# Out-projection of a decoder layer: its last two weight groups by seven block products of half width, sums on the vector engine

## The chip, the cores and the metric

One core of one Trainium2 chip runs the kernel. The engines named below are PE (TensorE, matmuls; PEld its weight loads), DVE (VectorE), ACT (ScalarE), POOL (GpSimd) and SP (SyncE, here only a DMA queue). The metric is the device time of one execution in microseconds; lower is better.

## The reference, cut to what matters

A layer takes `x` (512 tokens, 1024 features), normalises and modulates it, projects it, runs two head groups of attention, gates their outputs by SiLU, and projects back:

```python
y = jnp.concatenate([o_a.reshape(Bn, S, D_A) * jax.nn.silu(z_a.astype(jnp.float32)),
                     o_b.reshape(Bn, S, D_B) * jax.nn.silu(z_b.astype(jnp.float32))], axis=-1)
out = y.astype(x.dtype) @ w_out
return x + gate[:, None, :] * out
```

`y` is 512 x 1024, `w_out` 1024 x 1024, all float32. Only the product `y @ w_out` is computed in another way by the change. Everything ahead of it (input projection, sliding-window attention of group A, compressed, selected and windowed attention of group B) stays.

## The kernel before

Everything is held transposed: features on the 128 partitions, tokens along the free axis. `y` is eight tiles of 128 features x 512 tokens, `w_out` is cut into four weight groups `o0` to `o3` of 256 output features, each loaded as two halves of 512 KB (`load_next`, on SP's queue, one load for each `raw` buffer that comes free). The result is eight output tiles n = 0 to 7 of 128 features x 512 tokens.

Float32 accuracy comes from splitting each factor into a high part, rounded to the matmul's fp32r type, and a low part, the rest: `h = wh + wl`. The high part is an ACT copy, the low part a DVE subtraction (`split` for weights, L176 and L177; `make_y` for y, L810 and L811). A product is then three matmuls: wh by yh, wh by yl, wl by yh.

A weight group is split into four pieces of 128 x 512. `split_to` emits the splits six pieces ahead of the one that the matmuls use (`AHEAD`). `unit_col` makes one output tile: for each of the eight row tiles k of y, three matmuls of a 128 x 128 weight with 512 moving columns, accumulated in one PSUM bank; two pieces serve one output tile. The three banks of `PJ` take turns. After an output tile DVE computes `fin` = bank * gate + x (L1037), where x comes by a DMA on ACT's queue (`xr`), and SP stores it. The last tile, n=7, is done in two halves of 256 tokens so that the store behind the last matmul is short:

```python
for tok in ((slice(0, S),) if n < 7 else (slice(0, 256), slice(256, S))):
```

The y tiles 0 to 3 belong to head group A and are ready early. Tiles 4 to 7 belong to group B: `make_y` for row r runs when the attention of row r ends, or, where the gate of that row was not ready at that time, after all attention (the loop behind `stream.drain()`), from a copy `ob`.

The order of the work on each engine is not the order of the source text. A scheduler takes the instructions with their dependences and, in a simulated run, gives each engine the earliest one in the text whose inputs and buffers are ready. On the chip every engine then runs its own list in that fixed order and waits in front of an instruction whose inputs are late. Buffers come from pools: `t2` (tiles of 128 x 512, `NT2` of them: h, q, transposed probabilities, y), `rawp` (loaded weights), `pw` (split weights), and small ones (`W2`) for temporaries and `fin`.

## Time and profile before

| | |
|---|---|
| median of 3 runs | 311.42 us (311.38 to 311.58) |
| the profiled execution | 312.03 us on the device, span 309.4 us from the first to the last instruction |
| granted TensorE clock | 0.999 |
| busy | PE 302.0 us (98% of the span), PEld 255.2 (82%), DVE 241.6 (78%), ACT 194.9 (63%) |
| chain that ended last | PE 78%, DVE 11%, ACT 4%, DMA 3% |

The profile is one execution. A row of the timeline gives start, length, engine, line, operation and tiles (written from read); square brackets behind it give the idle time of the engine ahead of it and what released it. Lengths of matmuls overlap, since they are pipelined; the distance from start to start is the pace. A row of groups by shape has the count, the busy time, the mean length in ns, and the idle time ahead of the group. A row of stretches gives the busy time of each engine between two times of the span, then the granted clock, the DMA share and GB/s.

### The profile page before, as it was taken

Reading aid. Unit: us, or ns where it says so; the run is one execution under the profiler, and the core shown is the slowest. Engines: PE = TensorE matmul, PEld = TensorE weight load, DVE = VectorE, ACT = ScalarE, POOL = GpSimd, SP = SyncE. Lnnn points to the kernel's source line nnn. Section 1 sums busy time; section 2 is a strip of 40 time slices with the busy share of each in tenths; the row PEclk is TensorE's granted clock in tenths of the full one; section 3 lists DMA queues with packets and bytes.
Section 4 is the critical chain, followed back from the end, with each engine's and each line's share of the span. In section 5 each row is a group of like instructions: output and inputs, shape, how many; then the busy total and the mean of one; then the engine's idle time right before and its main releaser. Section 6 shows DMA issues by size and latency. Waiting matters only on the chain.

```text
span 309.4 us, 5849 instructions
## 1 busy us (share of the span) xinstructions
PE 302.0 (98%) x2119; PEld 255.2 (82%) x2119; DVE 241.6 (78%) x666; ACT 194.9 (63%) x472; POOL 4.1 (1%) x22
## 2 busy tenths in 40 slices
PE   8999999999999999999999999999999999999995
PEld 3678888788988999889887888888888888788885
DVE  5679998999967567898999999988789696544221
ACT  5686448668967675676936665869778877422000
POOL 0000000000000000000000000000000000000000
PEclk9999999999999999999999999999999999999999
DMA  7999969800390909170454004140420220254101
GB/s 252 382 407 408 406 202 251 307 0 0 117 328 13 293 4 263 45 271 2 154 182 158 20 2 138 65 138 3 136 71 0 68 70 2 68 172 135 68 34 68
DMA packets 28231, 44.11 MB, mean 143 GB/s; under 512 B 1787, under 2 KB 19612, under 8 KB 28204
## 3 DMA queue, kind: packets, MB, share of 16 engines
q1 hardware_dynamic: 26908, 41.57, 39.3%
q10 hardware_dynamic: 1296, 2.18, 2.3%
q8 instruction: 16, 0.26, 0.3%
q14 instruction: 11, 0.09, 0.1%
HBM read 41.61 MB, written 2.14 MB: 141 GB/s over the span
## 4 chain that ended last, share of the span: by engine, by line
PE 78%; DVE 11%; ACT 4%; DMA 3%; issue 1%; SPq 1%; DVEq 0%; ACTq 0%
PE pj L484 28%; PE po L949 8%; PE sq L292 8%; PE pj L474 8%; PE s L874 7%; PE pt L932 4%; PE skv L293 4%; PE pt L922 3%; PE s L603 3%; DVE qs L535 2%; DMA raw<-in_w_gate 2%; DVE raw L709 2%; DMA xTp<-in_xT 2%; DVE wl L177 1%; PE s L666 1%
## 5 line engine op out<-in xcount | busy, mean ns | idle before, releaser
L176 ACT ACTIVATE wh<-raw 128x512 fp32r<-128x512 f32 (+1 forms) x52 | 31.3, 635 | 18.0 <-PE pj L484 14.1
L474 PE MATMUL pj<-wl,hh 128*128 128x256 f32 (+1 forms) x128 | 36.8, 288 | 0.1
L474 PE MATMUL pj<-wh,hh 128*128 128x256 f32 (+1 forms) x128 | 37.0, 289 | 0.0
L474 PE MATMUL pj<-wh,hl 128*128 128x256 f32 (+1 forms) x128 | 36.5, 285 | 0.0
L177 DVE TENSOR_TENSOR wl<-raw,wh 128x512 fp32r<-128x512 f32 (+1 forms) x52 | 34.9, 690 | 1.8 <-ACT wh L176 1.7
L886 ACT ACTIVATE pp<-pp,nm 128x256 f32<-128x256 f32 (+2 forms) x48 | 29.3, 615 | 7.0 <-DVE nm L879 6.9
L484 PE MATMUL pj<-hl,wh 128*128 128x512 f32 x80 | 32.2, 402 | 0.0
L484 PE MATMUL pj<-hh,wl 128*128 128x512 f32 x80 | 32.0, 400 | 0.0
L484 PE MATMUL pj<-hh,wh 128*128 128x512 f32 x80 | 32.0, 400 | 0.0
L879 DVE CUSTOM_DVE_ANT_0 pp<-s,bias 128x256 f32<-128x256 f32 (+2 forms) x48 | 25.6, 553 | 4.1 <-PE s L874 3.6
L484 PE MATMUL pj<-yh,wl 128*128 128x512 f32 (+1 forms) x72 | 26.6, 370 | 0.0
L484 PE MATMUL pj<-yl,wh 128*128 128x512 f32 (+1 forms) x72 | 26.6, 369 | 0.0
L1037 DVE SCALAR_TENSOR_TENSOR fin<-pj,gate,xr 128x512 f32<-128x512 f32 (+1 forms) x9 | 6.2, 692 | 25.9 <-PE pj L484 25.9
L484 PE MATMUL pj<-yh,wh 128*128 128x512 f32 (+1 forms) x72 | 26.4, 371 | 0.0
L474 PEld LDWEIGHTS pj<-wl,hh 128*128 128x128 f32 x128 | 24.1, 188 | 0.6 <-DVE wl L177 0.3
L874 PE MATMUL s<-kTb,qs 128*128 128x256 f32 (+2 forms) x96 | 24.3, 356 | 0.0
L474 PEld LDWEIGHTS pj<-wh,hl 128*128 128x128 f32 x128 | 24.1, 188 | 0.2 <-issue 0.2
L474 PEld LDWEIGHTS pj<-wh,hh 128*128 128x128 f32 x128 | 24.1, 189 | 0.1
L907 DVE TENSOR_SCALAR pp<-pp,rr,grev 128x256 f32<-128x256 f32 (+2 forms) x48 | 21.0, 475 | 0.5
L933 ACT COPY ptT<-pt 128x384 f32<-128x384 f32 (+1 forms) x32 | 15.8, 528 | 6.0 <-PE pt L932 5.9
L534 ACT ACTIVATE qs<-pt 64x512 fp32r<-64x512 f32 x16 | 9.5, 592 | 13.4 <-PE pt L529 7.3
L484 PEld LDWEIGHTS pj<-hh,wh 128*128 128x128 f32 x80 | 15.1, 188 | 3.0 <-issue 0.2
(238 smaller groups left out, 721.4 us busy)
## 6 DMA issues: line engine op xcount, KB each, us to landing
ada_ring<-in_w_ada_rows SPq DMA_DIRECT2D x12, 512.0 KB, 7.2
raw<-in_w_cmp SPq DMA_DIRECT2D x8, 512.0 KB, 5.4
raw<-in_w_gate SPq DMA_DIRECT2D x8, 512.0 KB, 5.6
raw<-in_w_o SPq DMA_DIRECT2D x8, 512.0 KB, 4.2
wst_ring<-in_w_qkv_a SPq DMA_DIRECT2D x8, 384.0 KB, 7.7
xTp<-in_xT SPq DMA_DIRECT2D x8, 256.0 KB, 4.6
bias<-line_d SPq DMA_DIRECT2D x8, 256.0 KB, 4.1
raw<-in_w_q_b SPq DMA_DIRECT2D x4, 512.0 KB, 6.5
```

The lines of the kernel that those rows point to most:

```text
L176: ACT.activation(wh, src, AF.Copy)
L177: DVE.tensor_tensor(wl, src, wh.bitcast(F32), op=OP.subtract)
L292: PE.matmul(pj_q[tb], lt, w[:, 0:512], start=f, stop=l, skip_group_check=True)
L293: PE.matmul(pj_kv[tb // 2][:, tb % 2, :], lt, w[:, 512:768], start=f and tb % 2 == 0, stop=l, skip_group_check=True)
L474: PE.matmul(bank[:, t * n:(t + 1) * n], h[:, tb * 128:(tb + 1) * 128], w[:, k % 2, :], start=k == 0 and m == 0, stop=k == 7 and m == 2)
L484: PE.matmul(bank, w, h[:, tok], start=k == 0 and m == 0, stop=k == 7 and m == 2)
L874: PE.matmul(ps, qs[h][:, 128 * i:128 * i + 128], k[:, hl_, lo:lo + w], start=hl_ == 0, stop=hl_ == 1)
L879: DVE.tensor_tensor_reduce(out=P[:, g, 0:w], in0=ps, in1=bt, scale=1.0, scalar=init, op0=OP.add, op1=OP.min, accum_out=nm[:, g:g + 1])
L886: ACT.activation(P[:, g, 0:e], P[:, g, 0:e], AF.Exp, bias=nm[:, g:g + 1], scale=-1.0, accum_out=dn[:, g:g + 1])
L907: DVE.tensor_scalar(v, v, rr[:, g:g + 1], gates[:, g, br:br + 1], op0=OP.mult, op1=OP.mult)
L933: ACT.copy(T[:, 0:nb, :], rev(pt[:, 0:nb * 128].rearrange("p (b q) -> p b q", b=nb)))
L949: PE.matmul(o[64 * g:64 * g + 64, 128 * i:128 * i + 128], vb[:, 64 * g:64 * g + 64], sl["T"][g][:, b, :], start=first_of and b == 0, stop= ...
```

## The change

The groups `o2` and `o3` (output tiles 4 to 7) are computed by a two-by-two block scheme with seven products in place of eight. Split are the tokens (two halves of 256), the rows of y (tiles 0 to 3 and 4 to 7), and the output features of the group (two tiles of 128). So each weight group has four blocks of 512 rows x 128 features, held as 128 x 512 tiles (`11`, `12`, `21`, `22`), and y has four blocks of 512 rows x 256 tokens. Four of the products take sums of y blocks (`s1` to `s4`) and differences of weight blocks (`t1` to `t4`):

- `split_out` makes the pieces of a weight group in the order 11, t1, t2, 22, t3, 21, t4: for the t pieces one DVE subtraction of 128 x 512, then for every piece the high part on ACT and the low part on DVE. There are seven pieces for a group instead of four.
- `y_sums` is called for each of four rows r behind output tile 1 (for s1 and s2) and behind output tile 2 (for s3 and s4): two DVE operations of 128 x 256, an ACT high part and a DVE low part of 128 x 512. For this `yf` is kept, in pool `t2`.
- `out_product` runs 4 rows x 3 matmuls with 256 moving columns into one of three PSUM banks, r, v and w. Products that belong to the same running sum go on accumulating in the bank after it has been read: r takes four products (11·11, s2·t2, s3·t3, 22·t4), v two (s1·t1, s4·22), w one (12·21).
- Behind each product DVE adds its bank, times the gate, to half an output tile (256 tokens): seven such evictions for a group, four of them onto `xr` (the first for each of the four half-tiles), three onto what the half-tile already holds. Four stores of 128 KB for a group.
- Output tiles 0 to 3 are computed as before. The split of n=7 is gone with the tile's old form. `NT2` goes from 40 to 44, there is a pool `ot` of two 128 x 512 tiles for the differences, and `xr` has four buffers.
- The host layout of `w_o2` and `w_o3` puts each block in one contiguous piece; the bytes are the same.

```diff
@@ -26,7 +26,7 @@
 LINE = 640
 GW = 280
 AHEAD = 6
-NT2 = 40
+NT2 = 44
 WAIT_L, WAIT_M = 4, (0, 8)
 PER_A, PER_B = 3.6, (3.5, 1.6, 7)
 NEAR = 256
@@ -89,6 +89,7 @@
     t2 = ctx.enter_context(tc.tile_pool(name="t2", bufs=NT2))
     rawp = ctx.enter_context(tc.tile_pool(name="rawp", bufs=5))
     pw = ctx.enter_context(tc.tile_pool(name="pw", bufs=4))
+    ot = ctx.enter_context(tc.tile_pool(name="ot", bufs=2))
     sm = ctx.enter_context(tc.tile_pool(name="sm", bufs=2))
 
     def T2(dt, name):
@@ -153,18 +154,43 @@
             t = rawp.tile([128, 4, GW], F32, name="raw")
             if g[:4] == "gate":
                 raws[g, h] = t.rearrange("p a b -> p (a b)")[:, 0:D]
+            elif g in OUT:
+                raws[g, h] = t.rearrange("p a b -> p (a b)")[:, 0:D]
             else:
                 raws[g, h] = t[:, :, 0:A["w_" + g].shape[3]]
             SP.dma_start(raws[g, h], A["w_" + g][h])
 
-    COL = ("kv_cmp", "z_a0", "z_a1", "z_b0", "z_b1", "o0", "o1", "o2", "o3")
+    COL = ("kv_cmp", "z_a0", "z_a1", "z_b0", "z_b1", "o0", "o1")
+    OUT = ("o2", "o3")
+    BLOCKS = ("11", "t1", "t2", "22", "t3", "21", "t4")
     split_list = [(g, p) for g in ("kv_cmp", "kv_sel", "kv_win_g", "q_b0", "q_b1", "z_a0", "z_a1", "z_b0", "z_b1",
-                                   "o0", "o1", "o2", "o3") for p in range(4)]
+                                   "o0", "o1") for p in range(4)]
+    split_list += [(g, p) for g in OUT for p in BLOCKS]
     split_pos = {e: n for n, e in enumerate(split_list)}
     split_done = [0]
 
+    def split_out(g, p):
+
+        blocks = {f"{i + 1}{j + 1}": raws[g, i][:, 512 * j:512 * j + 512] for i in range(2) for j in range(2)}
+        wh, wl = (pw.tile([128, 2 * GW], F32R, name=n)[:, 0:512] for n in ("wh", "wl"))
+        if p in blocks:
+            src = blocks[p]
+        else:
+            a, b = {"t1": ("12", "11"), "t2": ("22", "t1"), "t3": ("22", "12"), "t4": ("21", "t2")}[p]
+            sums = raws[g, "t"] = raws.get((g, "t"), {})
+            src = sums[p] = ot.tile([128, 512], F32, name="ot")
+            DVE.tensor_tensor(src, *({**blocks, **sums}[n] for n in (a, b)), op=OP.subtract)
+        ACT.activation(wh, src, AF.Copy)
+        DVE.tensor_tensor(wl, src, wh.bitcast(F32), op=OP.subtract)
+        pieces[g, p] = [t.rearrange("p (k n) -> p k n", k=4) for t in (wh, wl)]
+        if p in ("t3", "t4"):
+            load_next()
+
     def split(g, p):
 
+        if g in OUT:
+            split_out(g, p)
+            return
         if g in COL:
             src = raws[g, p % 2][:, :, 128 * (p // 2):128 * (p // 2) + 128]
         else:
@@ -183,7 +209,7 @@
 
         while split_done[0] < min(len(split_list), split_pos[g, p] + ahead + 1):
             n, q = split_list[split_done[0]]
-            if not all((n, h) in raws for h in ((0, 1) if n in COL else (q // 2,))):
+            if not all((n, h) in raws for h in ((0, 1) if n in COL + OUT else (q // 2,))):
                 break
             split(n, q)
             split_done[0] += 1
@@ -800,15 +826,39 @@
         else:
             sz[n - 4] = z
 
-    yh, yl = {}, {}
+    yf, yh, yl, yp, sums_y = {}, {}, {}, {}, {}
+    TOK = (slice(0, 256), slice(256, 512))
+
+    def high_low(src, names):
+
+        h, l = (T2(F32R, n) for n in names)
+        ACT.activation(h, src, AF.Copy)
+        DVE.tensor_tensor(l, src, h.bitcast(F32), op=OP.subtract)
+        return h, l
 
     def make_y(c, o, z):
 
-        yf = W2("yf")
-        DVE.scalar_tensor_tensor(yf, o, 0.5, z, op0=OP.mult, op1=OP.mult)
-        yh[c], yl[c] = T2(F32R, f"yh{c}"), T2(F32R, f"yl{c}")
-        ACT.activation(yh[c], yf, AF.Copy)
-        DVE.tensor_tensor(yl[c], yf, yh[c].bitcast(F32), op=OP.subtract)
+        yf[c] = T2(F32, "yf")
+        DVE.scalar_tensor_tensor(yf[c], o, 0.5, z, op0=OP.mult, op1=OP.mult)
+        yh[c], yl[c] = high_low(yf[c], (f"yh{c}", f"yl{c}"))
+
+    def y_sums(r, second):
+
+        (a0, a1), (b0, b1) = ([yf[c][:, t] for t in TOK] for c in (r, 4 + r))
+        if not second:
+            s12 = sums_y[r] = T2(F32, "s12")
+            DVE.tensor_tensor(s12[:, TOK[0]], a1, b1, op=OP.add)
+            DVE.tensor_tensor(s12[:, TOK[1]], s12[:, TOK[0]], a0, op=OP.subtract)
+            src, names = s12, ("s1", "s2")
+            for n, c, e in (("11", r, 0), ("12", 4 + r, 0), ("22", 4 + r, 1)):
+                yp[n, r] = [x[c][:, TOK[e]] for x in (yh, yl)]
+        else:
+            src, names = W2("s34"), ("s3", "s4")
+            DVE.tensor_tensor(src[:, TOK[1]], b0, sums_y[r][:, TOK[1]], op=OP.subtract)
+            DVE.tensor_tensor(src[:, TOK[0]], a0, a1, op=OP.subtract)
+        t = high_low(src, ("ysh", "ysl"))
+        for n, e in zip(names, TOK):
+            yp[n, r] = [x[:, e] for x in t]
 
     def gen2():
         posts.append(cmp_attn())
@@ -1021,21 +1071,52 @@
     with in_order(tc, late, ACT.engine):
         xrs = []
         for n in range(2):
-            xrs.append(mp.tile([128, S], F32, name="xr", tag="qc", bufs=2))
+            xrs.append(mp.tile([128, S], F32, name="xr", tag="qc", bufs=4))
             ACT.dma_start(xrs[n], A["xT"][n])
-    for n in range(8):
+    for n in range(4):
         if n < 2:
             xr = xrs[n]
         else:
-            xr = mp.tile([128, S], F32, name="xr", tag="qc", bufs=2)
+            xr = mp.tile([128, S], F32, name="xr", tag="qc", bufs=4)
             ACT.dma_start(xr, A["xT"][n])
-        f = W2("fin")
-        for tok in ((slice(0, S),) if n < 7 else (slice(0, 256), slice(256, S))):
-            b = PJ()[:, tok]
-            for _ in unit_col(f"o{n // 2}", n % 2, b, (yh, yl), tok):
-                pass
-            DVE.scalar_tensor_tensor(f[:, tok], b, gate[:, n:n + 1], xr[:, tok], op0=OP.mult, op1=OP.add)
-            SP.dma_start(out[n][:, tok], f[:, tok])
+        f, b = W2("fin"), PJ()
+        for _ in unit_col(f"o{n // 2}", n % 2, b, (yh, yl)):
+            pass
+        DVE.scalar_tensor_tensor(f, b, gate[:, n:n + 1], xr, op0=OP.mult, op1=OP.add)
+        SP.dma_start(out[n], f)
+        if n in (1, 2):
+            for r in range(4):
+                y_sums(r, n == 2)
+
+    def out_product(g, bank, src, w, new):
+
+        split_to(g, w, AHEAD)
+        wh, wl = pieces[g, w]
+        for r in range(4):
+            h, l = yp[src, r]
+            for m, (p, q) in enumerate(((wh, h), (wh, l), (wl, h))):
+                PE.matmul(bank, p[:, r, :], q, start=new and r == 0 and m == 0, stop=r == 3 and m == 2,
+                          skip_group_check=True)
+
+    PRODUCTS = (("r", "11", "11", True, (0, 0, 0, False)), ("v", "s1", "t1", True, (1, 1, 0, False)),
+                ("r", "s2", "t2", False, (1, 0, 0, False)), ("v", "s4", "22", False, (1, 0, 1, True)),
+                ("r", "s3", "t3", False, (1, 1, 1, True)), ("w", "12", "21", True, (0, 0, 1, True)),
+                ("r", "22", "t4", False, (0, 1, 0, True)))
+    for q in range(2, 4):
+        g = OUT[q - 2]
+        xr, f = [], []
+        for n in (2 * q, 2 * q + 1):
+            xr.append(mp.tile([128, S], F32, name="xr", tag="qc", bufs=4))
+            ACT.dma_start(xr[-1], A["xT"][n])
+            f.append(W2("fin"))
+        part = {"r": PJ()[:, 0:256], "v": ps_s.tile([128, 512], F32, name="s")[:, 0:256], "w": PT()[:, 0:256]}
+        for p, src, w, new, (ch, t, more, done) in PRODUCTS:
+            out_product(g, part[p], src, w, new)
+            n = 2 * q + ch
+            DVE.scalar_tensor_tensor(f[ch][:, TOK[t]], part[p], gate[:, n:n + 1], (xr, f)[more][ch][:, TOK[t]],
+                                     op0=OP.mult, op1=OP.add)
+            if done:
+                SP.dma_start(out[n][:, TOK[t]], f[ch][:, TOK[t]])
 
 
 def _layout(inp):
@@ -1066,7 +1147,8 @@
     rows = np.concatenate([pair(r) for r in range(4)] + [512 + pair(r) for r in range(4)])
     wo = g("w_out")[0][rows].reshape(8, 128, 4, 256)
     for q in range(4):
-        a[f"w_o{q}"] = halves(wo[:, :, q].transpose(1, 0, 2))
+        a[f"w_o{q}"] = halves(wo[:, :, q].transpose(1, 0, 2)) if q < 2 else cc(
+            wo[:, :, q].reshape(2, 4, 128, 2, 128).transpose(0, 2, 3, 1, 4).reshape(2, 128, D))
     for n, name in enumerate(("w_cmp_k1", "w_cmp_v1")):
         a[f"w_cmp{n}"] = cc(g(name)[0].reshape(4, 4, 128, 256).transpose(0, 2, 1, 3))
     eye = np.eye(128, dtype=np.float32)
```

## The prediction

> **What bounds the kernel now.** I read the head of the page first, then its chain of waits, then the timeline of the end, because the change touches nothing but the out-projection there.
>
> ```profile
> span 309.4 us, 5849 instructions
> PE 302.0 (98%) x2119; PEld 255.2 (82%) x2119; DVE 241.6 (78%) x666; ACT 194.9 (63%) x472; POOL 4.1 (1%) x22
> PE 78%; DVE 11%; ACT 4%; DMA 3%; issue 1%; SPq 1%; DVEq 0%; ACTq 0%
> 264.31 41.95 PE pj L484 x204
> 306.26 0.03 issue
> 306.28 0.48 DVE fin L1037
> ```
>
> PE is busy for 98% of the span, and the chain ends with 41.95 us of nothing but out-projection matmuls (`unit_col`), one last `fin` on DVE, and its store. Whatever shortens PE's row of matmuls after 264 us shortens the kernel, as long as PE never waits. The pace of PE is read from starts, not from the modelled durations:
>
> ```profile
> 283.70 0.39 PE L484 MATMUL pj<-yh,wh 128*128 128x512 f32 x1
> ...
> 300.19 0.39 PE L484 MATMUL pj<-yh,wl 128*128 128x512 f32 x1
> 300.42 0.28 PE L484 MATMUL pj<-yh,wh 128*128 128x256 f32 x1
> ...
> 305.97 0.28 PE L484 MATMUL pj<-yh,wl 128*128 128x256 f32 x1
> ```
>
> 283.70 is the first matmul of output tile n=4, 300.42 the first of n=7, which is already done in two halves of 256 tokens. 72 matmuls of 512 columns take 300.42 - 283.70 = 16.72 us, 0.2322 us each; 48 of 256 columns start over 305.97 - 300.42 = 5.55 us, 5.55/47 = 0.1181 us each. Half the columns cost half the time (2 x 0.1181 = 0.2362), though each has a weight load of its own. The four tiles n=4 to 7 take 16.72 + 48 x 0.1181 = 22.39 us of PE.
>
> The engine that gets the new work is DVE, so I looked at how it stands in the same stretch:
>
> ```profile
> core 0: us, PE busy (x) PEld busy (x) DVE busy (x) ACT busy (x) POOL busy (x), PEclk, DMA share, GB/s
> 268.00:283.70 15.70, 15.70 (x70) 12.65 (x69) 5.90 (x10) 4.56 (x8) 0.00 (x0) 1.00 0.49 161
> 283.70:306.30 22.60, 22.54 (x121) 19.13 (x119) 6.51 (x11) 0.63 (x1) 0.00 (x0) 1.00 0.17 64
> DVE fin L1037 <- PE pj L484: 25.9, 9, 4.2
> ```
>
> DVE works 5.90 of 15.70 us and 6.51 of 22.60 us; its only large wait is `fin` for PE, 25.9 us over nine times. The granted clock is 1.00 in both stretches.
>
> **The change, part by part.** First what PE loses. Weight groups o2 and o3 (n=4 to 7) become 2 x 7 products of 4 rows x 3 matmuls, 256 columns each: 168 x 0.1181 = 19.84 us against 22.39. That is 2.55 us off PE, and off the end if PE is never kept waiting. The number of matmuls grows from 120 to 168, and so does the number of weight loads; the n=7 rows above already have one load for each 256-column matmul at 0.1181 us, so the loads add nothing beyond that pace.
>
> The Trainium skill (TensorE: Matmul & The Clock Gate, Back-to-back issue gap) would say otherwise: it gives a sustained 81 ns for a 128-column matmul with its load and 131 ns for 512, so a straight line between, an estimate from that page, makes a 256-column one 98 ns and not half of 131. By it the old part would be 72 x 131 + 48 x 98 ns = 14.1 us and the new 168 x 98 ns = 16.5 us, 2.3 us slower. The rows here do not agree: 232 and 118 ns, a ratio of 0.51, with 48 samples of the narrow form.
>
> Now what DVE gains in work. Its prices, by distance from one start to the next in an unbroken run:
>
> ```profile
> 266.15 1.89 DVE L811 TENSOR_TENSOR yl<-yf,yh 128x512 fp32r<-128x512 f32 x3
> 267.96 0.69 DVE L177 TENSOR_TENSOR wl<-raw,wh 128x512 fp32r<-128x512 f32 x1
> 270.40 0.75 DVE L1037 SCALAR_TENSOR_TENSOR fin<-pj,gate,xr 128x512 f32<-128x512 f32 x1 [1.75 <-PE pj L484]
> 271.07 0.68 DVE L177 TENSOR_TENSOR wl<-raw,wh 128x512 fp32r<-128x512 f32 x1
> 272.95 0.75 DVE L1037 SCALAR_TENSOR_TENSOR fin<-pj,gate,xr 128x512 f32<-128x512 f32 x1 [1.20 <-PE pj L484]
> 273.62 1.28 DVE L177 TENSOR_TENSOR wl<-raw,wh 128x512 fp32r<-128x512 f32 x2
> 278.32 0.75 DVE L1037 SCALAR_TENSOR_TENSOR fin<-pj,gate,xr 128x512 f32<-128x512 f32 x1 [3.43 <-PE pj L484]
> L671 DVE TENSOR_TENSOR pa<-pa,s 128x256 f32<-128x256 f32 x4 | 1.7, 414 | 0.0
> L1037 DVE SCALAR_TENSOR_TENSOR fin<-pj,gate,xr 128x256 f32<-128x256 f32 x2 | 1.0, 484 | 4.4 <-PE pj L484 4.4
> ```
>
> A subtraction of 512 columns takes (1.89 - 0.69)/2 = 0.60 us, a full `fin` 271.07 - 270.40 = 0.67. For 256 columns no unbroken run stands alone; the same 0.08 to 0.09 us taken off 0.414 and 0.484 gives 0.33 and 0.40. From 267.96, when the last y half is done, DVE has to do:
> - three `wl` of o1: 1.8 us; `fin` of n=0 to 3: 2.7 us (both as before)
> - `y_sums`, two calls for each of four rows, each two 256-column sums and one 512-column low part, 2 x 0.33 + 0.60 = 1.26: 10.1 us, all new
> - per weight group seven low parts and four block differences, 11 x 0.60 = 6.6, and seven evictions of 256 columns, 2.8: 9.4 us, 18.8 for both
>
> Together 33.4 us. PE from 267.96 to its last product has 283.70 - 267.96 + 19.84 = 35.6 us. DVE goes from a third busy to 94%: it does not become the bound on the sum, but it has hardly any slack in order.
>
> So the order decides. A product lasts 12 x 0.1181 = 1.42 us; numbering them P1 to P7, P3 is due at 283.70 + 2 x 1.42 = 286.54. P3 writes the same PSUM bank as P1, so it waits for the eviction of P1. That eviction is emitted after nearly everything: three `wl` 1.8, four `fin` 2.7, both `y_sums` 10.1, the blocks 11, t1, t2, 22 (3.6 with their differences), and t3 and 21 (1.8). That is 20.0 us from 267.96, so 287.96, and with its own 0.40 us 288.4: P3 is 1.8 us late. If t4 (1.2) also comes ahead, 3.0 late. P6 uses a third bank, and a scheduler that puts ready work first can run it in P3's place, which covers 1.42 of it: 0.4 late. For the stall of PE I take the middle of 0.4 and 3.0, 1.7 us. Later products have 1.42 us each for 1.34 us of DVE (9.4/7), so they add little.
>
> ACT gets six more `wh` and eight high parts of the sums; it was busy 4.56 of 15.70 and 0.63 of 22.60 us, and at the length of a row
>
> ```profile
> 266.81 2.18 ACT L176 ACTIVATE wh<-raw 128x512 fp32r<-128x512 f32 x4
> 281.42 1.14 ACT L176 ACTIVATE wh<-raw 128x512 fp32r<-128x512 f32 x2
> 306.79 0.33 SPq L1038 DMA_DIRECT2D out_dram<-fin  x1
> ```
>
> (2.18/4 = 0.55 us each) 14 x 0.55 = 7.7 us fit beside PE. If that cover were gone it would lengthen the wait for `wl`, not PE directly. DMA: the same eight loads of `xr` on ACT's queue, weights of the same size, and eight stores of 128 KB for two of 128 and three of 256 on SP, whose queue holds nothing else by then except the last weight load; I cost that at nothing, and at most one more issue of 0.33 us (row above) if two stores meet at the end. The end is unchanged: one 256-column eviction and one 128 KB store follow the last matmul in both kernels. More buffers (`t2` 44, `ot`, `xr` 4) cost no time unless they shift the earlier schedule; that is bounded by nothing in the trace, and I allow 0.5 us to either side. `yf` moves from the small pool into `t2`; eight tiles live longer, four more are there.
>
> Sum: -2.55 + 1.7 = -0.85 us. The profiled execution took 312.03 us on the device for its span of 309.4; it would come to 311.2. The median of the runs is 311.42, 0.6 us lower, and the same difference gives 310.57, so 310.6 us. A change of 0.2%, 0.6 us, is about what a measurement of this kernel can tell from none.
>
> **The rivals.**
>
> DVE covers everything. It has a gap before the last tiles of y:
>
> ```profile
> 264.35 0.69 DVE L808 SCALAR_TENSOR_TENSOR yf<-po,szb 128x512 f32<-128x512 f32 x1 [3.26 <-PE po L955]
> 264.95 1.28 DVE L808 SCALAR_TENSOR_TENSOR yf<-ob,szb 128x512 f32<-128x512 f32 x2
> ```
>
> In those 3.26 us one or two rows of `y_sums` (1.26 per call) could run, since some rows of y are complete earlier. That takes up to 2.5 us out of the 20.0 and P3 is on time; the stall is 0 to 0.7 and the time 308.9 to 309.6. Against it: the two `yf` of 264.95 read an `ob` made long before and still came only after the wait, so the order written by the scheduler did not fill this gap before.
>
> The gain is eaten: stall of 2 to 3.2 us, within 0.2%. This is the upper end of my bound, P3 held to about 3.0, with P6 not brought forward.
>
> DVE's order makes it slower. DVE runs its queue in order: at 270.40 it idled 1.75 us in front of `fin` although the `wh` for the next `wl` was done by 268.99 (266.81 + 2.18). If the sums are queued behind the first two `fin`, they start at 273.62, not 267.96. Of the 20.0 us, the two `wl` and two `fin` before that are done (2.5), 17.5 remain, and P1's eviction ends at 273.62 + 17.5 + 0.4 = 291.5: P3 5.0 us late, 3.6 with P6 in its place. With the middle, 4.3, the time is 311.42 - 2.55 + 4.3 = 313.2. It decides from the point where PE's stall passes 2.55 us, which by the same sum is 0.75 us of idle DVE between 268 and 288 (2.2 with P6 forward); it was idle 9.8 us of 15.7 there before, but had nothing else to do.
>
> Weight loads set the pace. There are 48 more of them, and each is recorded as
>
> ```profile
> L484 PEld LDWEIGHTS pj<-yl,wh 128*128 128x128 f32 x40 | 7.5, 188 | 1.1
> ```
>
> If a product could go no faster than one such load after the other, 168 x 0.188 = 31.6 us would stand for 22.39 and the time would be 320.6. The 48 narrow matmuls of n=7 speak against it: each had its own load and they came every 0.118 us, so loads overlap. The Trainium skill's figures cited above (TensorE: Matmul & The Clock Gate) lean the same way, with a smaller price.
>
> **How the numbers follow.** Forecast, gain with a stall of 0.7 to 1.9 us (309.6 to 310.8): 0.35. DVE covers everything: 0.18. Gain eaten (310.8 to 312.0): 0.23. Slower by DVE's order: 0.23. Weight loads at the pace: 0.01. Faster is 0.35 + 0.18 = 0.53, same 0.23, slower 0.24. The range goes from the whole gain, 311.42 - 2.55 = 308.9, to a stall of 4.5, 313.4, which leaves out the worst of the slower cases. The forecast's own range is 309.6 to 310.8.
>
> **What would show it.** 168 narrow matmuls at 0.118 us apart inside a product; if they stand at 0.13 or more, the PE term is wrong. Gaps of PE at the start of P3 or P4 of the first group, released by DVE (an eviction or the low part of a sum), 1 to 2 us in all; a gap of 4 us there is the slower rival, none is the better one. DVE near 90% busy from 268 us on. The wait of DVE for PE at `fin`, 25.9 us, down to a few us. The start of the first out-projection tile moving by more than 0.5 us from 264 would mean that the buffers shifted the earlier schedule, which I left out of the sum.

## The result, and the profile after

The kernel with the change takes 314.79 us (median of six runs, 313.61 to 315.47), the kernel before 311.46 us beside it (311.15 to 312.61): a ratio of 1.0098, 95% interval 1.0076 to 1.012. It is slower by about 3.1 us. The prediction was 310.6 us, with a range up to 313.4; of its cases the nearest is the slower one, by DVE's order (313.2 us, chance 0.23).

The profiled execution took 315.34 us for a span of 313.4 us (before: 312.03 for 309.4). The head of its page, with the row of granted clocks in 40 slices:

```profile
span 313.4 us, 6006 instructions
PE 302.7 (97%) x2167; PEld 258.8 (83%) x2167; DVE 262.5 (84%) x713; ACT 203.4 (65%) x486; POOL 4.2 (1%) x22
PEclk9999999999999999999999999999999999999599
PE 76%; DVE 14%; DMA 4%; ACT 3%; issue 2%; SPq 1%; POOL 0%; ACTq 0%; DVEq 0%; POOLq 0%
```

PE is as busy as before (302.7 against 302.0 us), although by its pace it has 2.55 us less to do. The digit 5 near the end says why: in one slice of 7.8 us the mean clock was little over half. Cut into stretches, the out-projection of after reads (columns as in the prediction: busy time by engine, clock, DMA share, GB/s):

```profile
core 0: us, PE busy (x) PEld busy (x) DVE busy (x) ACT busy (x) POOL busy (x), PEclk, DMA share, GB/s
264.45:283.89 19.44, 19.44 (x85) 15.77 (x84) 16.70 (x32) 8.60 (x15) 0.00 (x0) 1.00 0.32 109
283.89:286.72 2.83, 2.83 (x25) 2.78 (x23) 2.83 (x8) 1.17 (x2) 0.00 (x0) 1.00 0.00 0
286.72:290.93 4.21, 1.05 (x6) 0.68 (x4) 4.21 (x8) 1.88 (x4) 0.00 (x0) 0.82 0.38 125
290.93:296.25 5.32, 5.32 (x26) 5.32 (x26) 2.97 (x7) 1.78 (x3) 0.00 (x0) 0.50 0.00 0
296.25:310.14 13.89, 13.85 (x117) 13.65 (x116) 10.13 (x20) 2.94 (x5) 0.00 (x0) 1.00 0.17 59
```

Output tiles 0 to 3 take 19.44 us (19.55 before). Products 1 and 2 run at full pace. Then PE stands from 286.72, while DVE has no free moment (4.21 of 4.21 us), and when PE resumes it is busy for 5.32 us at a clock of 0.50. From 296.25 on all is well again, with DVE at 73%. In PE's timeline the hole and the slow stretch look like this:

```profile
283.89 0.28 PE L1098 MATMUL pj<-yh,wh 128*128 128x256 f32 x1
...
286.60 0.28 PE L1098 MATMUL s<-ysh,wl 128*128 128x256 f32 x1
288.72 0.38 PE L1098 MATMUL pt<-yh,wh 128*128 128x256 f32 x1 [1.84 <-ACT wh L183]
288.94 0.28 PE L1098 MATMUL pt<-yl,wh 128*128 128x256 f32 x1
290.55 0.58 PE L1098 MATMUL pt<-yh,wl 128*128 128x256 f32 x1 [1.32 <-DVE wl L184]
290.93 0.41 PE L1098 MATMUL pt<-yh,wh 128*128 128x256 f32 x1
291.14 0.41 PE L1098 MATMUL pt<-yl,wh 128*128 128x256 f32 x1
...
296.25 0.29 PE L1098 MATMUL s<-ysh,wl 128*128 128x256 f32 x1
```

`pt` is the bank of product 12·21, the sixth in the text: the scheduler put it third. Its first matmul waits for the high part of piece 21 (ACT), its third for the low part (DVE). From start to start, less the pace of 0.118 us, the two holes are 288.72 - 286.60 - 0.12 = 2.00 and 290.55 - 288.94 - 0.12 = 1.49 us, 3.49 together.

The account of the span, 309.4 to 313.4 us:

| | us |
|---|---|
| out-projection starts at 264.45, not 264.15 | +0.30 |
| output tiles 0 to 3 | -0.11 |
| 168 narrow matmuls for the old four tiles, at the pace of 0.118 us | -2.55 |
| two holes of PE | +3.49 |
| matmuls at less than full clock behind them | +2.73 |
| last `fin` to the end of the span (3.12, now 3.26) | +0.14 |
| sum | +4.00 |

In some executions of most of these kernels, the one before among them, the time is some 3 to 6 us longer at a lower mean clock (in the profile of e2_order below the granted clock is 0.68 from 8 to 24 us), so the profiles are compared by the time from the first out-projection matmul behind the attention to the last `fin`, and the ratios leave out the executions that are over 1.5% above the fastest of their kernel.

DVE's timeline from the end of the attention to the first eviction of a block product shows what PE waited for:

```profile
264.64 0.69 DVE L842 SCALAR_TENSOR_TENSOR yf<-po,szb 128x512 f32<-128x512 f32 x1 [3.25 <-PE po L1005]
266.03 0.69 DVE L836 TENSOR_TENSOR yl<-yf,yh 128x512 fp32r<-128x512 f32 x1 [0.70 <-ACT yh L835]
...
268.64 0.69 DVE L842 SCALAR_TENSOR_TENSOR yf<-ob,szb 128x512 f32<-128x512 f32 x1
270.02 0.69 DVE L836 TENSOR_TENSOR yl<-yf,yh 128x512 fp32r<-128x512 f32 x1 [0.70 <-ACT yh L835]
270.63 0.42 DVE L850 TENSOR_TENSOR s<-yf 128x256 f32<-128x256 f32 x1
...
286.73 0.69 DVE L182 TENSOR_TENSOR ot<-raw 128x512 f32<-128x512 f32 x1
...
289.80 0.70 DVE L184 TENSOR_TENSOR wl<-raw,wh 128x512 fp32r<-128x512 f32 x1
290.40 0.70 DVE L182 TENSOR_TENSOR ot<-raw,ot 128x512 f32<-128x512 f32 x1
291.00 0.49 DVE L1116 SCALAR_TENSOR_TENSOR fin<-pj,gate,xr 128x256 f32<-128x256 f32 x1
```

The first sum starts at 270.63, not at 267.96 as the prediction had it: the last three tiles of y are made one after the other, and two of their low parts wait 0.70 us for the high part, while a `wl` fills the third wait. The low part of piece 21 is at 289.80, and product 1 is evicted only at 291.00. The high part of 21 is late on ACT, although this block needs no difference:

```profile
286.19 1.30 ACT L835 ACTIVATE ysh<-s 128x512 fp32r<-128x512 f32 x2 [1.24 <-DVE s L858]
287.52 0.63 ACT L183 ACTIVATE wh<-ot 128x512 fp32r<-128x512 f32 x1
288.05 0.61 ACT L183 ACTIVATE wh<-raw 128x512 fp32r<-128x512 f32 x1
```

The row at 288.05 is piece 21. It stands in ACT's list behind two high parts of sums, which wait for DVE, and behind the high part of t3, whose difference DVE makes at 286.73. So both holes lead back to DVE's list.

### The profile page after: what moved, and what is told of

Same layout as the page of the kernel before. It is cut to its first block, busy times and chain, and to the rows that moved or that the text cites. A ratio compares the mean times of both kernels' runs of the same rounds, so it can differ in the third digit from the quotient of the medians.

```text
span 313.4 us, 6006 instructions
## 1 busy us (share of the span) xinstructions
PE 302.7 (97%) x2167; PEld 258.8 (83%) x2167; DVE 262.5 (84%) x713; ACT 203.4 (65%) x486; POOL 4.2 (1%) x22
## 4 chain that ended last, share of the span: by engine, by line
PE 76%; DVE 14%; DMA 4%; ACT 3%; issue 2%; SPq 1%; POOL 0%; ACTq 0%; DVEq 0%; POOLq 0%
PE pj L510 21%; PE pj L500 9%; PE sq L318 8%; PE s L924 7%; PE po L999 6%; PE pt L982 4%; PE skv L319 4%; PE pj L1098 4%; PE pt L972 3%; PE s L629 3%; DMA xTp<-in_xT 2%; DVE qs L561 2%; PE s L1098 1%; DVE kTb L579 1%; DMA raw<-in_w_o 1%
## 5 line engine op out<-in xcount | busy, mean ns | idle before, releaser
L203 DVE TENSOR_TENSOR wl<-raw,wh 128x512 fp32r<-128x512 f32 (+1 forms) x44 | 29.7, 690 | 1.8 <-ACT wh L202 1.7
L202 ACT ACTIVATE wh<-raw 128x512 fp32r<-128x512 f32 (+1 forms) x44 | 26.6, 636 | 0.1
L929 DVE CUSTOM_DVE_ANT_0 pa<-s,bias,nsink 128x256 f32<-128x256 f32 (+1 forms) x32 | 14.3, 449 | 4.0 <-POOL pa L933 2.4
L510 PEld LDWEIGHTS pj<-hh,wl 128*128 128x128 f32 x80 | 15.0, 188 | 2.9
L510 PEld LDWEIGHTS pj<-hl,wh 128*128 128x128 f32 x80 | 15.0, 188 | 2.8 <-issue 0.2
L924 PEld LDWEIGHTS s<-kTb,qs 128*128 128x128 f32 x96 | 15.8, 189 | 1.3
```

Of the source, the lines that this page charges most:

```text
L202: ACT.activation(wh, src, AF.Copy)
L203: DVE.tensor_tensor(wl, src, wh.bitcast(F32), op=OP.subtract)
L510: PE.matmul(bank, w, h[:, tok], start=k == 0 and m == 0, stop=k == 7 and m == 2)
L924: PE.matmul(ps, qs[h][:, 128 * i:128 * i + 128], k[:, hl_, lo:lo + w], start=hl_ == 0, stop=hl_ == 1)
L929: DVE.tensor_tensor_reduce(out=P[:, g, 0:w], in0=ps, in1=bt, scale=1.0, scalar=init, op0=OP.add, op1=OP.min, accum_out=nm[:, g:g + 1])
```

## The experiments

In the table, first is the start of the first out-projection matmul behind the attention, holes are distances between matmul starts over 0.3 us beyond the pace, and slow is the sum of the smaller excesses. Some matmuls of the out-projection run ahead of that mark: fifteen in e8 and e13, eleven in e7, e1b, e3 and e11, twelve in the others. Each makes the time to the last `fin` 0.232 us shorter. The device time is the median of all executions.

| kernel | first | to last `fin` | holes | slow | device, us | ratio to before (95%) |
|---|---|---|---|---|---|---|
| before | 264.15 | 42.13 | 0 | 0 | 311.46 | |
| after | 264.45 | 45.69 | 3.49 | 2.73 | 314.79 | 1.0098 (1.0076 to 1.012) |
| e1_no_sums | 267.29 | 39.89 | 0 | 0.31 | 309.98 | 0.9941 (0.9905 to 0.9977) |
| e2_order | 267.90 | 44.71 | 3.46 | 1.74 | 314.43 | 1.0115 (1.005 to 1.018) |
| e2_filled | 264.52 | 44.58 | 1.21, and 3.76 filled | 0.15 | 314.25 | 1.0086 (1.0057 to 1.0114) |
| e8_yfpool | 264.67 | 45.00 | 3.49 | 2.65 | 316.31 | 1.0143 (1.007 to 1.0217) |
| e5_pool_sums | 264.39 | 42.65 | 2.28 | 0.83 | 312.72 | 1.0034 (0.9993 to 1.0075) |
| e7_pool_both | 268.68 | 44.79 | 3.27 | 1.74 | 317.61 | 1.0197 (1.0145 to 1.025) |
| e9_late34 | 265.54 | 45.44 | 5.00 | 0.87 | 315.51 | 1.0134 (1.0097 to 1.0171) |
| e1b_no_diffs | 263.18 | 42.32 | 2.01 | 0.41 | 310.89 | 0.9986 (0.9948 to 1.0024) |
| e3_buffers | 263.20 | 42.35 | 0 | 0 | 310.68 | 0.9983 (0.9946 to 1.0021) |
| e4_one_group | 269.00 | 40.77 | 0 | 0 | 311.96 | 1.0005 (0.9975 to 1.0034) |
| e11_one_late | 263.20 | 41.03 | 0 | 0 | 309.70 | 0.9945 (0.9912 to 0.9979) |
| e13_one_late_yfpool | 264.74 | 40.02 | 0 | 0 | 309.88 | 0.9959 (0.9927 to 0.9991) |

The theory behind the first runs: DVE, delayed by the sums, opens a hole of PE, and the hole drops the clock. The rival: the narrow products are themselves slower than the sum has them, whatever DVE does.

**e1_no_sums.** The sums of y are not made; halves of y tiles take their place, and the output is not the layer's.

```diff
+        if not second:
+            for n, c, e in (("11", r, 0), ("12", 4 + r, 0), ("22", 4 + r, 1),
+                            ("s1", r, 0), ("s2", r, 1), ("s3", 4 + r, 0), ("s4", 4 + r, 1)):
+                yp[n, r] = [x[c][:, TOK[e]] for x in (yh, yl)]
+        return
```

> Leaves out the sums of y blocks: s1 to s4 are replaced by plain halves of y tiles that exist already, so the products have the same shapes and the output is not the layer's. It takes 16 sums of 256 columns and 8 low parts off DVE, 10.1 us. Theory 1 (DVE's backlog, mostly the sums, holds back the split of the weight pieces and the evictions, and PE waits 3.5 us for them): no gap of PE over 0.5 us behind 283 us, granted clock 1.00 throughout, and nearly the whole 2.55 us of PE gained: 308.9 to 309.5 us. Rival (products that accumulate in one bank wait for each other's evictions whatever DVE has to do, or narrow matmuls are dear): gaps of PE between products remain, 311.5 us or more.

Its stretch from product 1 to the last `fin`:

```profile
286.80:307.18 20.38, 20.34 (x169) 19.95 (x167) 16.20 (x30) 4.74 (x8) 0.00 (x0) 1.00 0.15 53
```

No hole, clock 1.00, PE busy for 20.34 of 20.38 us: 168 matmuls at 0.118 us would be 19.84. The total of 39.89 us is 2.24 under before. The rival falls: what was lost behind product 2 goes when the sums go. Two reservations: the device time, 309.98 us, is a little over the 308.9 to 309.5 expected, and the order on PE changed as well, since without the sums the scheduler left product 3 in third place.

**e2_order and e2_filled.** Both write the order of the group's products on PE out (11, t1, 21, t2, 22, t3, t4, the order that after has), and the second puts 16 matmuls of 512 columns, whose result is not used, into the hole.

```diff
+                with in_order(tc, {PE.engine: mark[0]}, PE.engine):
+                    spare = ps_o.tile([128, 512], F32, name="po")
+                    for _ in range(FILL):
+                        PE.matmul(spare, pieces["o2", "11"][0][:, 0, :], yh[0], start=True, stop=True)
+                    product(part["w"], "12", *pieces[g, "21"], True)
...
+    FILL = 16
```

> The changed kernel with only the order of products on PE written out for group o2 as the profile shows it (11, t1, 21, t2, 22, t3, t4). It is the control for e2_filled. Both theories: as the changed kernel, 314 to 315.5 us, a gap of about 3.5 us behind the second product and a granted clock of 0.5 for some 6 us behind it.

> As e2_order, with 16 matmuls of 512 columns (16 x 0.232 = 3.7 us, result not used) in PE's list behind the second product, in the gap. Theory 2 (the idle gap is what halves the granted clock for the next 24 matmuls, and that costs some 2.4 us of its own): granted clock 1.00 all through, products behind the gap at 0.118 us a matmul, 2 to 2.5 us less than e2_order, so 312 to 313 us, though the gap's own 3.5 us stay. Rival (the clock falls for another reason, the narrow matmuls or their bursts): clock 0.5 again, time as e2_order or up to 0.4 us more.

Stretches of e2_order from its hole on, then of e2_filled:

```profile
290.20:294.00 3.80, 0.65 (x5) 0.31 (x3) 3.80 (x8) 1.85 (x4) 0.00 (x0) 1.00 0.43 137
294.00:296.00 2.00, 2.00 (x10) 2.00 (x11) 2.00 (x5) 1.20 (x3) 0.00 (x0) 0.54 0.01 2
296.00:312.60 16.60, 16.57 (x134) 16.37 (x133) 11.42 (x22) 3.53 (x6) 0.00 (x0) 0.95 0.14 49
```

```profile
286.79:292.00 5.21, 4.16 (x21) 3.20 (x19) 5.21 (x11) 2.90 (x6) 0.00 (x0) 1.00 0.31 101
292.00:309.10 17.10, 17.06 (x142) 16.86 (x142) 12.02 (x23) 3.71 (x7) 0.00 (x0) 1.00 0.14 48
```

With the hole filled the clock stays at 1.00. From the third matmul of product 12·21 to the last `fin` e2_filled takes 17.10 us, e2_order 312.61 - 293.99 = 18.62 and after 310.14 - 290.55 = 19.59: the fall of the clock costs 1.5 to 2.5 us behind the hole. In e2_order the slow stretch is 3.5 us long, where some 6 were expected. But the whole was expected 2 to 2.5 us below e2_order, and the totals differ by 0.13 us (44.58 against 44.71), the device times not by more than their spread. In e2_filled the scheduler put the evictions of products 1 and 2 and a difference on DVE ahead of the low part of 21, so that the third matmul came at 292.00 - 283.96 = 8.04 us behind product 1, against 293.99 - 287.35 = 6.64 in e2_order. So the mechanism is shown by the clock row and the stretch, not by the device time.

**e8_yfpool.** The eight `yf` get a pool of their own.

```diff
-        yf[c] = T2(F32, "yf")
+        yf[c] = yfp.tile([128, S], F32, name="yf")
```

> The changed kernel with the eight yf tiles in a pool of their own instead of the shared t2 pool. Theory 3 (in the changed kernel the last three yf wait for a t2 buffer, so DVE does yf, yl, yf, yl with waits for ACT between and starts the sums 2.7 us late, at 270.6 instead of 268): the three yf follow each other, sums start at 268 to 269, PE's gap shrinks from 3.5 to 1 to 2 us; 310.5 to 312.8 us, the lower end if the clock then stays at 1.00. Rival (only the amount of work on DVE counts): gap within 0.7 us of the old one, 314 to 315.5 us.

DVE's timeline of it:

```profile
269.09 0.41 DVE L851 TENSOR_TENSOR s<-yf 128x256 f32<-128x256 f32 x1
270.66 0.69 DVE L837 TENSOR_TENSOR ysl<-s,ysh 128x512 fp32r<-128x512 f32 x1 [0.70 <-ACT ysh L836]
274.14 0.75 DVE L1086 SCALAR_TENSOR_TENSOR fin<-pj,gate,xr 128x512 f32<-128x512 f32 x1 [0.86 <-PE pj L511]
278.09 0.75 DVE L1086 SCALAR_TENSOR_TENSOR fin<-pj,gate,xr 128x512 f32<-128x512 f32 x1 [0.72 <-PE pj L511]
```

The sums start 1.5 us earlier (269.09; the out-projection itself is 0.2 us later than in after). Yet the holes are the same 3.49 us, as the rival had it. The 0.70 us in front of a low part stands in after too (at 272.21), but 0.86 and 0.72 us in front of `fin` for PE are new, 1.58 us together: as much as was won. An earlier start of the sums alone repairs nothing here, since the `fin` in DVE's list cannot be earlier than PE's tiles. The total of 45.00 is 0.69 under after, which is the three matmuls more ahead of the mark (3 x 0.232 = 0.70).

**e5_pool_sums and e7_pool_both.** The first moves the sixteen 256-column sums to POOL, the second the block differences as well.

```diff
-            DVE.tensor_tensor(s12[:, TOK[0]], a1, b1, op=OP.add)
+            POOL.tensor_tensor(s12[:, TOK[0]], a1, b1, op=OP.add)
...
-            DVE.tensor_tensor(src, *({**blocks, **sums}[n] for n in (a, b)), op=OP.subtract)
+            POOL.tensor_tensor(src, *({**blocks, **sums}[n] for n in (a, b)), op=OP.subtract)
```

> The sixteen 256-column sums on POOL, which is busy 4.2 us in the whole kernel; takes 16 x 0.33 = 5.3 us off DVE. No run shows the price of such a sum on POOL; the theory needs one under about 1.2 us. Theory 1: the gap of 3.5 us goes to 0 to 0.7 us and the clock stays at 1.00; first out-projection matmul to last eviction 39.5 to 40.5 us, device time 309.0 to 310.2. Rival (POOL is too slow, or slows DVE while both run): a gap of 2 us or more at the first product with a sum, 44 us or more, device time 313 or more.

> The sums and the eight block differences on POOL: 10.1 us off DVE. Theory 1: no gap, 39.4 to 40.2 us from first out-projection matmul to last eviction, 308.9 to 309.8 us; no better than e5_pool_sums by more than its gap. Rival (POOL's own list becomes the bound, at over 1.5 us for a 512-column difference): gaps at the t pieces, 42 us or more.

Groups on POOL of e5_pool_sums, and a row of its PE timeline; then a row of PE's timeline of e7_pool_both, and a stretch of it:

```profile
L858 POOL TENSOR_TENSOR s<-yf 128x256 f32<-128x256 f32 x4 | 4.9, 1218 | 0.0
L850 POOL TENSOR_TENSOR s<-yf 128x256 f32<-128x256 f32 x4 | 3.7, 922 | 141.6 <-DVE yf L842 141.6
```

```profile
289.34 0.36 PE L1098 MATMUL pj<-ysh,wh 128*128 128x256 f32 x1 [1.80 <-DVE fin L1116]
```

```profile
294.82 0.55 PE L1098 MATMUL pj<-ysh,wh 128*128 128x256 f32 x1 [2.64 <-DVE fin L1116]
```

```profile
294.80:299.00 4.20, 4.18 (x23) 4.20 (x24) 4.09 (x5) 1.89 (x4) 4.12 (x4) 0.62 0.00 1
```

A sum takes POOL 0.92 to 1.22 us, where one follows the other on DVE after 0.34 (280.70 to 281.04 in after). With them off DVE the hole of the narrow products shrinks to 1.96 us in one piece, now in front of product 3 for the eviction of product 1 (the other 0.32 of the table's 2.28 lies in the first output tiles), and the clock stays at full. The total is 42.65, 3.0 under after and 0.5 over before, between what the theory and the rival expected; the device time cannot be told from before. The gain is so small because DVE slowed down, a rival that the expectation named and these rows show: DVE's operation of 512 columns lasts 1.23 us while POOL is at its last sum (284.00 to 285.19), and the next one 0.68.

```profile
284.51 1.23 DVE L836 TENSOR_TENSOR ysl<-s,ysh 128x512 fp32r<-128x512 f32 x1
285.66 0.68 DVE L184 TENSOR_TENSOR wl<-ot,wh 128x512 fp32r<-128x512 f32 x1
```

In e5 DVE is busy for 262.9 us of the whole span with sixteen operations fewer, in after for 262.5: nothing came off it. With the differences on POOL too (1.6 us each) the theory fails altogether and the total is in the rival's range: DVE is busy for 263.2 us, and the eviction of product 1 is later again, with one hole of 2.81 us (2.64 of it recorded as idle), matmuls every 0.21 us for 3.1 us behind it (the 0.62 of the stretch mixes these with 1 us at full clock), and a ratio of 1.0197.

**e9_late34.** The second call of `y_sums` is moved behind product t1 of the first group.

```diff
-        if n in (1, 2):
+        if n == 1:
...
+            if q == 2 and w == "t1":
+                for r in range(4):
+                    y_sums(r, True)
```

> The changed kernel with the second call of y_sums (s3, s4) written behind the second product of group o2 instead of behind output tile 2, so that the evictions of the first products and the splits stand ahead of it; the same work on DVE. If the order of DVE's list makes the gap (the eviction and the low parts that the third product needs stand behind sums that are needed later), the gap falls to under 2 us in all and moves to the product that takes s4: 42 to 44 us from first out-projection matmul to last eviction, 311 to 313.2 us. If the amount of work alone counts, the gap is 3 us or more again and the time as the changed kernel's, 45 us and 314 us.

Two stretches of 6 us of it:

```profile
291.00:297.00 6.00, 4.22 (x29) 3.42 (x28) 6.00 (x15) 3.15 (x5) 0.00 (x0) 1.00 0.00 0
297.00:303.00 6.00, 4.75 (x38) 4.33 (x37) 6.00 (x13) 2.30 (x4) 0.00 (x0) 1.00 0.24 84
```

The eviction of product 1 is no longer behind all the sums (it is at 286.65, 1.6 us behind the product's start), but the sums now delay the later products: the idleness comes in seven pieces of 0.41 to 1.17 us, 5.00 in all, with DVE busy for 12.00 of 12.00 us. The clock stays at 1.00. The total is 45.44, 0.25 under after: the rival, that the amount of DVE's work in this stretch counts and not where the sums stand, is nearer. What was gained on the clock (slow 0.87 for 2.73) was lost in idleness (5.00 for 3.49).

**e1b_no_diffs.** The block differences are not computed; a block takes the place of each, and the output is not the layer's.

```diff
-            DVE.tensor_tensor(src, *({**blocks, **sums}[n] for n in (a, b)), op=OP.subtract)
+            src = blocks[{"t1": "12", "t2": "22", "t3": "12", "t4": "21"}[p]]
```

> Leaves out the block differences: t1 to t4 are plain weight blocks, so the output is not the layer's; 8 x 0.60 = 4.8 us off DVE, but of them only t3 and t4 of the first group (1.2 us) stood between the end of the attention and the gap; t1 and t2 had been made at 216 and 248 us. If what counts is the work queued on DVE ahead of the gap: gap 2.2 to 3.0 us instead of 3.5, 43.8 to 45 us from first out-projection matmul to last eviction (45.7 in the changed kernel). If the whole sum of DVE's work counts, the gap is 0 and this time 40 us. Both: the waits of DVE for a weight load at 216 and 248 us (0.58 and 1.27 us) are gone.

```profile
283.00:290.00 7.00, 5.48 (x41) 4.86 (x40) 7.00 (x16) 5.54 (x10) 0.00 (x0) 1.00 0.18 44
```

The holes are 0.68, 0.95 and 0.37 us, 2.0 in all, where 2.2 to 3.0 were expected, and the clock stays at 1.00, so the total is 42.32, below the 43.8 to 45 that were expected. So the differences have a part in the stall, but the sums have the larger one: without them no hole was left. And the out-projection starts at 263.18, 1.27 us earlier than in after. What stood in the way there is seen in the chain of waits of after and in DVE's timeline:

```profile
243.37 4.25 DMA raw<-in_w_o
247.63 0.69 DVE ot L182
```

```profile
247.63 0.69 DVE L182 TENSOR_TENSOR ot<-raw,ot 128x512 f32<-128x512 f32 x1 [1.27 <-DMA raw<-in_w_o]
```

A difference, t2, whose product is due behind 286 us, was put into the attention's work at 247, and DVE stood there for 1.27 us for a weight load, with the attention behind it.

**e3_buffers.** The kernel before with the change's buffers alone.

```diff
-NT2 = 40
+NT2 = 44
...
-        yf = W2("yf")
+        yf = T2(F32, "yf")
+        kept.append(yf)
```

> The kernel before with two of the change's side effects alone: yf kept in the shared t2 pool and NT2 44. Measures what the buffers do to the schedule: the last three yf and yl interleave with waits for ACT as in the changed kernel (0.70 us each). Theory: PE is not held by that, so the time stays within 0.5 us of before, 311.0 to 312.0 us, and the first out-projection matmul within 0.3 us of 264.15. Rival: the buffers cost a good part of the 3 us: 312.5 us or more.

Its first out-projection matmul behind the attention:

```profile
263.20 0.39 PE L484 MATMUL pj<-yh,wl 128*128 128x512 f32 x1
```

That is 0.95 us before the 264.15 of before, where no more than 0.3 either way was expected. So the +0.30 of the account is two things, as far as single profiles tell: the buffers give 0.95, and the differences put into the attention take 1.25 (0.72 and 1.02 if the one matmul more behind the mark of e3 is counted). On the device 0.9983 cannot be told from no change.

**e4_one_group, e11_one_late, e13_one_late_yfpool.** All use the block scheme for `o3` alone, so product 1 is due two output tiles, some 11 us, later. e11 also holds the pieces of the block scheme on DVE behind the last tile of y; e13 is e11 with the pool of e8.

```diff
-    OUT = ("o2", "o3")
+    OUT = ("o3",)
...
-    for n in range(4):
+    for n in range(6):
...
+    done_y[DVE.engine] = [i for i in tc.nc.cur_bb.bb.instructions if i.engine == DVE.engine][-1]
...
         if g in OUT:
-            split_out(g, p)
+            with in_order(tc, done_y, DVE.engine):
+                split_out(g, p)
```

> Only the last weight group o3 by blocks, o2 as before. DVE keeps the sums (10.1 us) but loses one group's 9.4 us for 2.4, and has two more wide output tiles (11.2 us of PE) to do it behind. Theory 1 (DVE's backlog makes the gap): no gap over 0.3 us, granted clock 1.00, half of the gain: from the first out-projection matmul behind the attention to the last eviction 41.97 - 1.27 = 40.7 us, device time 310.2 to 310.6. Rival (a gap at the change from wide to narrow products whatever DVE's load): 41.5 us or more, device time 311.4 or more.

> As e4_one_group (only o3 by blocks), and the block differences kept behind the last y tile in DVE's list. In e4_one_group DVE stood 1.07 us at 258.6 us, in the attention stage, in front of a difference whose weight load had not landed. Theory 4 (that wait is what took back part of e4's gain: 40.77 us against 42.13 in the out-projection, but 0 to 0.6 us on the device): the out-projection as in e4, 40.6 to 41.0 us, attention ends as in the kernel before, device time 309.8 to 310.4 us, clearly faster than before. Rival (the attention is not held by it): as e4_one_group, 310.5 to 311.5 us.

> As e11_one_late, with the yf tiles in a pool of their own, so that the last three yf follow one another. Theory: with one group DVE has slack, so this changes little: within 0.4 us of e11_one_late. Rival (late y tiles hold PE): 0.5 us or more faster than e11_one_late.

In e4 the total came out as expected, 40.77 us without a hole, but the device time did not, with a ratio of 1.0005 where 310.2 to 310.6 us were expected: a difference again stands in the attention, in front of a load.

```profile
258.59 0.69 DVE L182 TENSOR_TENSOR ot<-raw 128x512 f32<-128x512 f32 x1 [1.07 <-DMA raw<-in_w_o]
```

In e11 that is gone; its first matmul, the stretch of the seven products and the last eviction:

```profile
263.20 0.40 PE L512 MATMUL pj<-yh,wl 128*128 128x512 f32 x1
```

```profile
294.10:304.20 10.10, 10.10 (x85) 9.85 (x84) 6.57 (x12) 0.63 (x1) 0.00 (x0) 1.00 0.15 54
```

```profile
304.23 0.48 DVE L1119 SCALAR_TENSOR_TENSOR fin<-pj,gate,xr 128x256 f32<-128x256 f32 x1 [0.92 <-PE pj L1101]
```

The 84 narrow matmuls run in 10.10 us (84 x 0.118 = 9.9) at a clock of 1.00, with DVE at 65%. At 309.70 us, 0.9945 of before (0.9912 to 0.9979), e11 beats both kernels, by about half a per cent of the one before. e3, timed on the same chip, has the buffers alone at 310.68, and both start the out-projection at 263.20: from there e11 takes 42.35 - 41.03 = 1.32 us less, the half of 2.55 that one group can give. e13 is within 0.2 us of e11, as expected: its mark is 1.54 us later and its time from there 1.01 us shorter, of which 4 x 0.232 = 0.93 are the four matmuls more ahead of the mark.

## Why the prediction was wrong

**The PE term was right.** 168 matmuls at 0.118 us stand in place of 22.39 us; e1 shows 2.24 of the 2.55 us when nothing else interferes, and 48 more weight loads slowed nothing. The rival on weight loads is out.

**DVE's ledger was near in amount, wrong in time.** The prediction counted 20.0 us of work ahead of product 1's eviction. From the first sum to that eviction the trace has 291.00 - 270.63 = 20.37 us, 0.70 of it idle. Part of this agreement is luck: one `wl` of o1 and the differences of t1 and t2 (1.8 us) had been done earlier and the difference of t4 (0.6) came in, so that 18.8 us were left at the prediction's prices, and they took 19.67. The step "From 267.96" failed: it was read from the schedule of before, where the last `yf` follow one another. In after they alternate with their low parts, two of which wait 0.70 us for ACT, a `wl` stands among them, and the first sum came 2.67 us later. The shared pool made this order: with a pool of their own (e8) the `yf` follow one another again.

**The stall was mis-sized: 3.49 us, not 1.7.** The eviction was done at 291.40 instead of 288.4, 3.0 us later, and with the 0.4 of the better bound this would make 3.4. That it is near 3.49 is luck, for in after PE did not wait for the eviction at all: it waited for the pieces of 21, and even at 0.118 us a matmul the nine of this product from 290.55 on would have lasted to 290.55 + 9 x 0.118 = 291.61, past the eviction. PE waits for the eviction where product 3 stays in third place behind the sums (e5, e7). The middle of 1.7 us lay between the stalls of two orders, neither with any idleness of DVE in it, and the scheduler had chosen one.

**Product 6 forward was right, its cover was not.** It was run in the place of product 3, but its own pieces stood behind the sums as well: high part on ACT at 288.05, low part on DVE at 289.80. The prediction took it as ready work that covers 1.42 us of the stall; it was what PE waited for.

**The clock was missing from the sum.** I had read the clock as 1.00 in the stretch of before, where PE never stands, and carried it over to a kernel in which it does. It fell to 0.50 and cost some 2.6 of the 2.73 us in the row of the account, as much as the whole gain. This is the largest term that no step had.

**DMA and buffers were put at nothing, and both moved the start.** The buffers moved it by -0.95 us (e3), outside the 0.5 allowed, and the differences emitted ahead, one of them waiting for a load, moved it by +1.25 us; only their sum was small. The prediction costed what was added at the place where it is needed, not where a scheduler with a look-ahead of six pieces would put it.

**The rivals.** The slower case had the right engine and the right kind of failure, and its 313.2 us is 1.6 under the measured 314.79. Its start of the sums, 273.62, was too late, its stall of 4.3 us against 3.49 too long, and the clock was missing in it as well: two errors that partly cancel. "DVE covers everything" fell with the first sum at 270.63: none ran in the gap of 3.25 us before the last tiles. The gain eaten by a stall of 2 to 3.2 us misses the measured stall by 0.3 and the clock.

## What to carry to other kernels

When work is taken off a busy engine and put on another, cost the second engine's list up to each point where the first engine needs something of it, idle time included, with its latest start; a load of 94% over the whole stage says little. Here a stretch of DVE was all but full for 20 us, and neither an earlier start (e8) nor another order (e9) removed the stall; only less work in that stretch (e1, in part e1b) or more time ahead of it (e4, e11) did, and giving work to a third engine slowed the second (e5, e7). Look also at what the work brought forward needs itself. Then price any hole on the first engine at its length and at what follows it, and keep look-ahead work that waits for loads out of lists that feed something urgent. If the second engine has not the room, do the part of the change that fits, as e11 does: half the gain without a hole is worth more than the whole with one.

## What the runs showed of the hardware

A hole of PE has a second price. Behind holes of 2.00 and 1.49 us with two matmuls between (after, e2_order, e8) the granted clock fell to about half, and matmuls of 256 columns came every 0.21 us (291.14 - 290.93) in place of 0.118. The slow stretch lasted 5.7 us in after (290.55 to 296.25) and 3.5 in e2_order (293.99 to 297.45). One hole of 2.81 us, 2.64 of it recorded as idle, was enough in e7; one of 1.96 us (1.80 recorded as idle) in e5, and idleness in pieces up to 1.17 us in e9, left the clock at 1.00, and so did filling the hole with matmuls that nobody needs in e2_filled. The Trainium skill (TensorE: Matmul & The Clock Gate, Part 1: The HAM clock gate) says that the clock is halved after an idle window of some 3.4 us and comes back after about as long a busy one, the window running free. The half agrees (0.50); the recovery agrees in e2_order (3.5 us) and is longer in after (5.7); of idleness less in one piece sufficed here, 2.64 us. Where between holes of 1.96 and 2.81 us it begins, how two holes count together, and how far it hangs on where the window stands, these runs leave open.

POOL took 0.92 to 1.22 us for a sum of 256 columns (e5) and 1.6 us for a difference of 512 (e7), 2.7 to 3.6 times the 0.34 and 0.60 us after which one such operation follows the other on DVE. And the two slow each other. Of the eleven two-input operations of 512 columns that DVE ran in e5 wholly beside POOL's sums, ten took 0.99 to 1.26 us; beside an idle POOL they took 0.67 to 0.70, in all kernels here. `fin`, which reads PSUM, stayed at 0.74 to 0.75. Single sums on POOL lasted 0.73 to 1.30 us.
